# Second-type MLPs: up projections as seven products of quarter matrices, with weight sums made by accumulating DMAs

## Chip, cores and metric

The kernel runs on one core of a Trainium2 chip. The metric is the device time of one execution in microseconds (us). The engines are named as in the profile: PE multiplies matrices (PEld loads its weights), DVE, ACT and POOL do elementwise work, and SP and ACT issue DMAs. POOL issues some too in the changed kernel.

## What is computed

A block of the first type is followed by two layers of the second type, on 512 tokens with 1024 features, in float32. The change lies in the MLP of the second type:

```python
for l in range(DEPTH_2):                      # 2 layers
    ...                                       # attention, convolution, w_o
    h2 = _rmsnorm(x, g_ffn[l])
    z = _dwconv(h2 @ w_up[l], w_dw_ffn[l], b_dw_ffn[l])   # w_up: 1024 x 5632, conv of 3 taps over tokens
    zg, zv = jnp.split(z, 2, axis=-1)         # 2816 gate and 2816 value columns
    x = x + (jax.nn.silu(zg) * zv) @ w_down[l]            # w_down: 2816 x 1024
```

## The kernel before

Features lie on the 128 partitions and the 512 tokens along the free dimension: `x` is eight tiles of 128x512. A product with a weight block of 128x128 is three matmuls (`mm3`), since weights and inputs are each split into a high and a low part of the type that PE multiplies in one pass: `whi` with `xh`, `whi` with `xl`, `wlo` with `xh`.

**The weight stream.** The host packs all weights in the order of use into units of eight 128x128 blocks (`weight_plan`, `pack_weights`), 512 KB each. `take` hands out block after block. It prepares units (`prep`) up to three ahead of the one in use: SP loads `raw` (L356, three buffers), ACT casts it to `whi` (L357), POOL subtracts to get `wlo` (L358). `whi` and `wlo` have four buffers each. There are 301 units.

**The MLP.** The 22 columns of 128 gate features each pair with 128 value features. For each pair PE runs 2 projections of 8 blocks (`proj`), 48 matmuls of 512 columns. `conv3` multiplies the result by the norm's factor `r`, which is a row over tokens and so may come after the product (L1279). It then does the 3 taps (L1282 to L1284). Silu and the product of gate and value follow (L1298), then the split into `ah` and `al`. After 11 pairs (`CHUNK2`) come the 8 down projections of that chunk, each added to `x` (L1303). The first two pairs run as `proj_outer`, with four banks of PSUM open and the input tiles in the outer loop, because the inputs come one by one from the step before. The sum for the norm (`total`, L478) stands behind it, and `rsqrt` makes `r` from it (L342, L487 to L489). Layer 2's last chunk ends in `final`, which does the last two down projections in halves of 256 columns, with the last norm and the stores.

Tile pools give PSUM its eight banks in turn (`b`). A scheduler orders each engine's instructions ahead of time, and every engine runs its own in that order.

Of the kernel before, what the change touches and what calls it, by code (L numbers as in the profile page):

```python
# [39 lines left out]
NL = 2  # L40
# [6 lines left out]
CHUNK2 = 11  # L47
# [27 lines left out]
def _span(c0, n=P):  # L75
    return np.arange(c0, c0 + n)


def weight_plan():
# [47 lines left out]
    for l in range(NL):  # L127
# [31 lines left out]
        for c in range(NF2 // CHUNK2):  # L159
            fs = list(range(c * CHUNK2, (c + 1) * CHUNK2))  # L160
            if c == 0:
                add(outer("w_up_2", l, KT, [_span(P * f + o) for f in fs[:2] for o in (0, FF2)]))
                fs = fs[2:]
            for f in fs:
                add(tiles("w_up_2", l, k8, _span(P * f)))
                add(tiles("w_up_2", l, k8, _span(FF2 + P * f)))
            add([("w_down_2", l, P * k, _span(P * m)) for m in range(KT) for k in range(c * CHUNK2, (c + 1) * CHUNK2)])
# [3 lines left out]
def pack_weights(inputs, plan):  # L171
    out = np.zeros((len(plan), P, UNIT * P), np.float32)
    for u, blocks in enumerate(plan):
        for b, (name, l, r0, cols) in enumerate(blocks):
            w = inputs[name] if l is None else inputs[name][l]
# [4 lines left out]
    return out  # L180

# [70 lines left out]
class Kern:  # L252
    def __init__(self, tc, xT, w, vec, cst, pos, outT):
        self.tc, self.nc = tc, tc.nc
        self.xT, self.w, self.vec_d, self.cst_d, self.pos_d, self.outT = xT, w, vec, cst, pos, outT
        self.plan = weight_plan()
        self.units = {}
        self.prepped = 0
        self.cur, self.blk = 0, 0
        self.table, self.table_users = None, []  # L260


    def setup(self, ctx):
# [23 lines left out]
        nc.gpsimd.memset(self.epst, EPS)  # L287
        self.lna = {}
# [59 lines left out]
    def prep(self, u, eng=None):  # L348
        nc = self.nc
        n = len(self.plan[u]) * P  # L350
        raw = self.wp.tile([P, UNIT * P], F32, name="raw", bufs=3)
        hi = self.wp.tile([P, UNIT * P], FR, name="whi")
        lo = self.wp.tile([P, UNIT * P], FR, name="wlo")
        cuts = (0, n) if eng is None else (0, n // 2, n)
        for cs in map(slice, cuts, cuts[1:]):
            nc.sync.dma_start(out=raw[:, cs], in_=self.w[u, :, cs])  # L356
            nc.scalar.copy(out=hi[:, cs], in_=raw[:, cs])  # L357
            (eng or nc.gpsimd).tensor_tensor(out=lo[:, cs], in0=raw[:, cs], in1=hi[:, cs].bitcast(F32), op=ALU.subtract)  # L358
        self.units[u] = (hi, lo)

# [39 lines left out]
    def proj_outer(self, pool, tag, acts, n, parts=WHOLE, between=None):  # L400
# [3 lines left out]
        if len(parts) == 1:  # L404
            for k, a in enumerate(acts):
                for ps in pss:
                    self.mm3(ps, self.take(), a, k == 0, k == len(acts) - 1)
            return pss
# [82 lines left out]
    def norm_in(self, pool, gname, l, on_pool=KT - 2):  # L491
# [14 lines left out]
        def finish(pp, tag):  # L506
            r = self.rp.tile([P, S], F32, name="r", bufs=1)
            self.rsqrt(r, self.total(pp, tag, acc)[0], D)
            return r
# [470 lines left out]
    def layer2(self, l, carry=None):  # L980
# [294 lines left out]
        ffc = tc.tile_pool(name="ffc", bufs=CHUNK2, reuse_waits="tile")  # L1275
        fp = ffc.__enter__()

        def conv3(ps, f, tag):
            V.tensor_tensor(out=ps, in0=ps, in1=r, op=ALU.mult)  # L1279
            w3 = self.v("w_dw_ffn_2", l, 3 * f, 3)  # L1280
# [6 lines left out]
        for c in range(NF2 // CHUNK2):  # L1287
            a = []
            pss = []
            if c == 0:  # L1290
                pss = self.proj_outer(pp, "b", acts, 4)
                r = fin(pp, "b")
            for f in range(c * CHUNK2, (c + 1) * CHUNK2):
                pg, pv = pss[2 * f : 2 * f + 2] if 2 * f < len(pss) else (self.proj(pp, "b", acts), self.proj(pp, "b", acts))
                cg = conv3(pg, f, "cg")
                cv = conv3(pv, NF2 + f, "cv")
                self.act(AF.Silu, out=cg, in_=cg)
                V.tensor_tensor(out=cg, in0=cg, in1=cv, op=ALU.mult)  # L1298
                a.append(self.split(fp, cg, ("ah", "al")))
            tail = 2 if l == NL - 1 and c == NF2 // CHUNK2 - 1 else 0  # L1300
            for m in range(KT - tail):
                ps = self.proj(pp, "b", a)
                V.tensor_tensor(out=self.x[m], in0=self.x[m], in1=ps, op=ALU.add)  # L1303
            if tail:
                self.final(pp, a)
        self._close(ffc)
        self._close(xg)
        self._close(pp_)

# [39 lines left out]
def program(tc, xT, w, vec, cst, pos, outT):  # L1349
    from contextlib import ExitStack  # L1350

    with ExitStack() as ctx:
        k = Kern(tc, xT, w, vec, cst, pos, outT)
        k.setup(ctx)
        carry = k.block1()
# [5 lines left out]
def arrays(inputs):  # L1361
# [3 lines left out]
        "w": pack_weights(inputs, weight_plan()),  # L1365
        "vec": pack_vectors(inputs),
# [14 lines left out]
```

## Time and profile before

| | |
|---|---|
| median of 3 runs (range) | 1893.43 us (1893.03 to 1894.1) |
| the profiled execution | 1894.09 us, of which its span is 1892.4 us |
| PE busy | 1844.0 us, 97% of the span |
| DVE, ACT, POOL busy | 959.7, 948.1, 937.1 us, 51%, 50%, 50% |
| mean DMA rate | 87 GB/s |

Busy times of PE are those of overlapping matmuls: each is recorded with 0.39 us at 512 columns, while the next one starts earlier. So the distance of starts tells what PE needs, and the count of matmuls in a window tells how full it is. The second-type MLPs lie at 931 to 1291 us and at 1519 to 1876 us of the span.

### The profile page before, as it was taken

The numbers are of one execution on the slowest core, as the hardware profiler recorded it, in microseconds if no ns is written. First come the engines' busy times: TensorE is split into PE (matmuls) and PEld (weight loads), VectorE is DVE, ScalarE is ACT, GpSimd is POOL, SyncE is SP. The second block draws the span as 40 slices with busy tenths as digits, with TensorE's granted clock in tenths as the row PEclk, the third lists the DMA queues.
The fourth block names the chain that finished last, engine by engine and source line by source line (L and its number), as shares of the span: only waits on it lengthen the run. The fifth ranks groups of instructions, "written<-read, shape, count | busy, mean of one in ns | idle before, by whom it ended". The sixth has DMA issues, their size and how long they took to land. (4 is left out here: it accounts for less than half of the span.)

```text
span 1892.4 us, 22115 instructions
## 1 busy us (share of the span) xinstructions
PE 1844.0 (97%) x8448; PEld 1500.1 (79%) x8448; DVE 959.7 (51%) x1420; ACT 948.1 (50%) x1442; POOL 937.1 (50%) x510
## 2 busy tenths in 40 slices
PE   8999999999999999899999999999999999999997
PEld 6877888888888888666788888888866788888886
DVE  4666552724032038996565225522998365405543
ACT  6766633633233347597554224434778554324442
POOL 5233444644444558665544444455866464444442
PEclk9999999999999999999999999999999999999999
DMA  5111224222222222200232222222210122222221
GB/s 186 68 56 61 79 101 140 89 101 91 99 100 90 100 79 90 78 27 23 87 110 93 97 101 97 92 100 93 97 39 23 61 101 100 92 98 100 95 96 56
DMA packets 48649, 164.89 MB, mean 87 GB/s; under 512 B 5536, under 2 KB 7584, under 8 KB 48544
## 3 DMA queue, kind: packets, MB, share of 16 engines
q1 hardware_dynamic: 46304, 160.34, 24.5%
q10 hardware_dynamic: 2240, 3.15, 0.5%
q8 instruction: 66, 1.08, 0.2%
q14 instruction: 39, 0.32, 0.1%
HBM read 161.37 MB, written 2.10 MB: 86 GB/s over the span
## 5 line engine op out<-in xcount | busy, mean ns | idle before, releaser
L358 POOL TENSOR_TENSOR wlo<-raw,whi 128x1024 fp32r<-128x1024 f32 x300 | 720.7, 2404 | 817.5 <-ACT whi L357 813.6
L357 ACT CAST whi<-raw 128x1024 fp32r<-128x1024 f32 (+1 forms) x302 | 313.7, 1040 | 507.5 <-PE b L379 412.7
L378 PE MATMUL b<-xh,whi 128*128 128x512 f32 (+1 forms) x1296 | 495.3, 382 | 2.7 <-ACT xh L449 2.7
L379 PE MATMUL b<-xl,whi 128*128 128x512 f32 (+1 forms) x1296 | 491.7, 379 | 3.4 <-DVE xl L450 3.3
L380 PE MATMUL b<-xh,wlo 128*128 128x512 f32 (+1 forms) x1296 | 491.3, 379 | 0.0
L379 PEld LDWEIGHTS b<-xl,whi 128*128 128x128 f32 x1296 | 244.3, 189 | 51.6 <-DVE xl L450 4.4
L378 PEld LDWEIGHTS b<-xh,whi 128*128 128x128 f32 x1296 | 244.2, 188 | 50.4 <-ACT xh L449 3.1
L380 PEld LDWEIGHTS b<-xh,wlo 128*128 128x128 f32 x1296 | 244.3, 189 | 45.9
L378 PE MATMUL b<-ah,whi 128*128 128x512 f32 (+1 forms) x646 | 243.6, 377 | 0.0
L379 PE MATMUL b<-al,whi 128*128 128x512 f32 (+1 forms) x646 | 243.2, 377 | 0.0
L380 PE MATMUL b<-ah,wlo 128*128 128x512 f32 (+1 forms) x646 | 243.2, 376 | 0.0
L380 PEld LDWEIGHTS b<-ah,wlo 128*128 128x128 f32 x646 | 121.6, 188 | 22.4
L378 PEld LDWEIGHTS b<-ah,whi 128*128 128x128 f32 x646 | 121.6, 188 | 22.3
L379 PEld LDWEIGHTS b<-al,whi 128*128 128x128 f32 x646 | 121.6, 188 | 22.2
L1218 POOL TENSOR_TENSOR cacc<-cacc,pd 128x510 f32<-128x510 f32 (+14 forms) x94 | 120.4, 1281 | 32.0 <-ACT pd L1216 28.3
L1206 DVE SCALAR_TENSOR_TENSOR cv<-u,vec,cv 128x497 f32<-128x497 f32 (+13 forms) x146 | 108.3, 742 | 7.7 <-ACT cv L1196 5.5
L1279 DVE TENSOR_TENSOR b<-b,r 128x512 f32<-128x512 f32 x88 | 61.0, 697 | 97.1 <-PE b L380 96.9
L1303 DVE TENSOR_TENSOR x<-x,b 128x512 f32<-128x512 f32 x30 | 20.6, 687 | 161.3 <-PE b L380 161.3
L446 ACT CAST ah<-cg 128x512 fp32r<-128x512 f32 x44 | 27.3, 621 | 98.7 <-DVE cg L1298 98.7
L378 PE MATMUL mm<-xh,whi 128*128 128x512 f32 x176 | 69.4, 394 | 0.0
L869 DVE TENSOR_TENSOR b<-rl,b 128x512 f32<-128x512 f32 x32 | 22.1, 695 | 92.6 <-ACT rl L868 92.6
L379 PE MATMUL mm<-xl,whi 128*128 128x512 f32 x176 | 68.8, 391 | 0.0
(430 smaller groups left out, 2851.1 us busy)
## 6 DMA issues: line engine op xcount, KB each, us to landing
raw<-w SPq DMA_DIRECT2D x295, 512.0 KB, 3.2
x<-xT SPq DMA_DIRECT2D x8, 256.0 KB, 6.6
x<-xT ACTq DMA_DIRECT2D x8, 256.0 KB, 4.8
raw<-w SPq DMA_DIRECT2D x7, 256.0 KB, 2.6
outT<-o ACTq DMA_DIRECT2D x4, 256.0 KB, 2.4
outT<-o SPq DMA_DIRECT2D x4, 256.0 KB, 2.5
vec<-vec SPq DMA_DIRECT2D x1, 363.0 KB, 6.9
f<-pos SPq DMA_DIRECT2D x1, 256.0 KB, 3.3
```

What stands on the lines that cost most here:

```text
L357: nc.scalar.copy(out=hi[:, cs], in_=raw[:, cs])
L358: (eng or nc.gpsimd).tensor_tensor(out=lo[:, cs], in0=raw[:, cs], in1=hi[:, cs].bitcast(F32), op=ALU.subtract)
L378: mm(ps, lhsT=wb[0], rhs=xb[0], start=start, stop=False, **kw)
L379: mm(ps, lhsT=wb[0], rhs=xb[1], start=False, stop=False, **kw)
L380: mm(ps, lhsT=wb[1], rhs=xb[0], start=False, stop=stop, **kw)
L446: nc.scalar.copy(out=hi, in_=src)
L869: V.tensor_tensor(out=ps, in0=rl, in1=ps, op=ALU.mult)
L1206: V.scalar_tensor_tensor(out=acc[:, o], in0=us[i][:, u], scalar=self.v("w_dw_conv_2", l, i * CONV_K + k), in1=acc[:, o], op0=ALU.mult, op1 ...
L1218: G.tensor_tensor(out=acc[:, o], in0=acc[:, o], in1=pd, op=ALU.add)
L1279: V.tensor_tensor(out=ps, in0=ps, in1=r, op=ALU.mult)
L1303: V.tensor_tensor(out=self.x[m], in0=self.x[m], in1=ps, op=ALU.add)
```

## The change

For all but the first three pairs of a layer, gate and value are computed together. The weight of a pair is cut into four quarters (a11, a12, a21, a22: two halves of the 1024 inputs, gate and value), the normed input into B11 to B22 (two halves of the features, tokens 0 to 255 and 256 to 511). Seven products of 4 blocks by 256 columns and sums of them give the same four results as eight such products. Four weight sums are needed (S1 = a21 + a22, S2 = S1 + a11, S3 = a11 + a21, S4 = S2 + a12 in the signs of the packed quarters) and four input combinations (T1 to T4). The results come out with the value's sign turned, which the taps undo (`wneg`).

- **Weight sums.** They are made in DRAM, each in five regions of four pairs (the last of three): ACT issues a copy of one quarter or sum into the region, and POOL an accumulating DMA that adds another quarter. That is 80 DMAs of up to 1 MB: 40 per layer. One is issued behind the `whi` cast (copies) or the `wlo` subtraction (adds) of every second unit from unit 24 on for layer 0, then of every third unit from unit 105 on for layer 1, up to unit 222. Layer 0's quarter products begin with unit 147.
- **Weight stream.** A pair takes 28 blocks (3.5 units) where it took 16 (2 units); there are 359 units. Units that hold quarters or sums are loaded by two or more DMAs of 256 KB.
- **Inputs.** `norms` runs inside `proj_outer` before its fourth input tile; `r` is multiplied into the inputs, and `quarter_inputs` makes and splits the seven operands (14 casts on ACT, 6 subtractions on POOL, 24 instructions on DVE per layer). The first three pairs still use the plain inputs and multiply by `r` afterwards.
- **Products.** PE's order is written by hand. Between products three partial sums per pair are copied out by ACT (`snap`, 128x256) and added by DVE (`plus`, 128x256). `unit` writes into PSUM where `conv3`'s user wrote to SBUF.
- **Chunks.** Three of 8, 7 and 7 pairs instead of two of 11; the last pair's two late products stand between the first down products.

```diff
-CHUNK2 = 11
+CHUNKS2 = (0, 8, 15, 22)
+PLAIN2 = 3
+NDOWN = 3
+SUM_PAIRS = 4
+SIDE_FROM, SIDE_STEPS = 24, (2, 3)
...
+        if u >= SIDE_FROM and self.side and u % SIDE_STEPS[self.side[0][0]] == 0:
+            _, begin, on_pool = self.side.popleft()
+            self.issue_behind(begin(), rest if on_pool else cast)
...
+            def copy(dst, src):
+                return lambda: nc.scalar.dma_start(out=dst, in_=src)
+            def add(dst, src):
+                return lambda: nc.gpsimd.dma_start(out=dst, in_=src, accum_op=ALU.add, max_dma_last_dim=row)
...
+        pss = self.proj_outer(pp, "b", acts, 2 * OUTER2, between=norms)
+        pss += [self.proj(pp, "b", acts) for _ in range(2 * (PLAIN2 - OUTER2))]
...
-            V.tensor_tensor(out=ps, in0=ps, in1=r, op=ALU.mult)
...
+                def times(ps, name, start, stop):
+                    hi, lo = ops[name]
+                    for kk in range(KT // 2):
+                        self.mm3(ps, self.take(), (hi[:, kk], lo[:, kk]), ...)
+                def p4(g):
+                    times(g["v"][:, L], "T4", False, True)
+                    plus(g["v"][:, R], g["g"][:, R], g["u3"])
+                def p3(g):
+                    times(g["g"][:, R], "B22", False, True)
+                    plus(g["g"][:, R], g["g"][:, R], g["u2"])
+                    a.append(unit(g["f"], g["g"], g["v"], self.wneg[l][:, 3 * g["f"] : 3 * g["f"] + 3]))
...
+                    times(g["v"][:, L], "B11", True, False)
+                    u1 = snap(g["v"][:, L])
+                    times(g["g"][:, L], "B21", True, True)
+                    plus(g["g"][:, L], g["g"][:, L], u1)
+                    if old is not None:
+                        p4(old)
+                    times(g["v"][:, L], "T2", False, False)
+                    g["u2"] = snap(g["v"][:, L])
+                    times(g["g"][:, R], "T1", False, False)
+                    if old is not None:
+                        p3(old)
+                    times(g["v"][:, L], "T3", False, False)
+                    g["u3"] = snap(g["v"][:, L])
...
+                down(0, 4)
+                p4(old)
+                down(4, 8)
+                p3(old)
+                down(8, NDOWN * len(ks))
```

**PE, start of layer 0's MLP.** `acc_...,ones` is the norm's sum; the `b_...` are banks. Before, with the last of the outer projections ahead of it and the third pair behind:

```order
L380 MATMUL b_7870<-xh_7825,wlo_7874 128x512
L378 MATMUL b_7871<-xh_7825,whi_7873 128x512
L379 MATMUL b_7871<-xl_7826,whi_7873 128x512
L380 MATMUL b_7871<-xh_7825,wlo_7874 128x512
L478 MATMUL b_7993<-acc_7810,ones_115 128x512
L378 MATMUL b_8034<-xh_7811,whi_7903 128x512
```

Now:

```order
L478 MATMUL b_7987<-xh_7914,whi_7838 128x512
L479 MATMUL b_7987<-xl_7915,whi_7838 128x512
L480 MATMUL b_7987<-xh_7914,wlo_7839 128x512
L580 MATMUL b_8038<-acc_7909,ones_115 128x512
L478 MATMUL b_7984<-xh_7916,whi_7838 128x512
L479 MATMUL b_7984<-xl_7917,whi_7838 128x512
```

The sum moved from behind all 96 matmuls of the outer projections to behind the first 36 of them.

**DVE, the same place,** from the last step of `rsqrt` on. Before (layer 1's, which has the same shape) it goes over to the first pair at once:

```order
L489 SCALAR_TENSOR_TENSOR r_12561<-b_12562,r_12561 128x512
L1279 TENSOR_TENSOR b_12437<-b_12437,r_12561 128x512
L1279 TENSOR_TENSOR b_12438<-b_12438,r_12561 128x512
L1279 TENSOR_TENSOR b_12439<-b_12439,r_12561 128x512
L1283 SCALAR_TENSOR_TENSOR cg_12571<-b_12437,vec_67,cg_12571 128x511
```

Now (layer 0), the second half of `quarter_inputs` and what follows it, where `t`, `h0`, `h1` are the inputs' tiles and L1437 is the first `plus`:

```order
L1534 SCALAR_TENSOR_TENSOR t_8086<-t_8086,h1_8077 128x512
L1426 TENSOR_TENSOR b_7984<-b_7984,r_8037 128x512
L1426 TENSOR_TENSOR b_7985<-b_7985,r_8037 128x512
L1518 TENSOR_TENSOR T4l_7978<-t_8086,T4h_7977 128x512
L1426 TENSOR_TENSOR b_7986<-b_7986,r_8037 128x512
L1426 TENSOR_TENSOR b_7987<-b_7987,r_8037 128x512
L1426 TENSOR_TENSOR b_8175<-b_8175,r_8037 128x512
L1426 TENSOR_TENSOR b_8207<-b_8207,r_8037 128x512
L1404 SCALAR_TENSOR_TENSOR cg_8248<-b_7984,vec_67,cg_8248 128x511
L1404 SCALAR_TENSOR_TENSOR cv_8252<-b_7985,vec_67,cv_8252 128x511
L1437 TENSOR_TENSOR b_8296<-b_8296,snap_8317 128x256
```

Between `rsqrt` and the first `plus` of the first quarter pair DVE now has the 24 instructions of `quarter_inputs`, the six multiplications by `r` of the plain pairs and two taps.

**POOL, layer 0's last chunk.** Before there are only subtractions:

```order
L358 TENSOR_TENSOR wlo_8193<-raw_8191,whi_8192 128x1024
L358 TENSOR_TENSOR wlo_8224<-raw_8222,whi_8223 128x1024
L358 TENSOR_TENSOR wlo_8271<-raw_8269,whi_8270 128x1024
L358 TENSOR_TENSOR wlo_8302<-raw_8300,whi_8301 128x1024
L358 TENSOR_TENSOR wlo_8349<-raw_8347,whi_8348 128x1024
```

Now, with the adds for layer 1's sum S4:

```order
L404 TENSOR_TENSOR wlo_10742<-raw_10740,whi_10741 128x1024
L449 DMA S4_1_2_169<-wq 512x512
L404 TENSOR_TENSOR wlo_10780<-raw_10778,whi_10779 128x1024
L404 TENSOR_TENSOR wlo_10813<-raw_10811,whi_10812 128x1024
L404 TENSOR_TENSOR wlo_10846<-raw_10844,whi_10845 128x1024
L449 DMA S4_1_3_173<-wq 512x512
```

Every third subtraction is followed by an accumulating DMA of 512 rows of 512 numbers, which POOL issues before the next subtraction.

## Rows read from the trace of the kernel before

**Rows 1.** The page: busy time of each engine, its share, instructions.

```profile
PE 1844.0 (97%) x8448; PEld 1500.1 (79%) x8448; DVE 959.7 (51%) x1420; ACT 948.1 (50%) x1442; POOL 937.1 (50%) x510
```

**Rows 2.** Windows: layer 0's MLP, its up phase, layer 1's MLP; length, busy (count), clock, DMA.

```profile
core 0: us, PE busy (x) PEld busy (x) DVE busy (x) ACT busy (x) POOL busy (x), PEclk, DMA share, GB/s
931.30:1291.00 359.70, 359.70 (x1586) 297.57 (x1585) 157.77 (x211) 143.06 (x179) 172.99 (x76) 1.00 0.28 97
969.00:1051.00 82.00, 82.00 (x363) 67.92 (x362) 48.63 (x68) 37.36 (x49) 36.09 (x15) 1.00 0.28 97
...
1502.00:1862.00 360.00, 360.00 (x1588) 297.71 (x1587) 162.71 (x214) 146.17 (x184) 169.14 (x72) 1.00 0.27 94
```

**Rows 3.** Timeline of PE, first block: matmuls of 256 columns (start, length, what).

```profile
328.75 0.28 PE L378 MATMUL b<-mh,whi 128*128 128x256 f32 x1
...
330.79 0.28 PE L380 MATMUL b<-mh,wlo 128*128 128x256 f32 x1
330.91 0.28 PE L378 MATMUL b<-mh,whi 128*128 128x256 f32 x1
```

**Rows 4.** Groups by line with shapes apart: count, busy us, mean ns, idle before.

```profile
L357 ACT CAST whi<-raw 128x1024 fp32r<-128x1024 f32 x295 | 309.4, 1051 | 506.0 <-PE b L379 412.7 <-issue 44.7 <-PE mm L379 20.6
L358 POOL TENSOR_TENSOR wlo<-raw,whi 128x1024 fp32r<-128x1024 f32 x295 | 714.1, 2423 | 802.1 <-ACT whi L357 802.0
L358 POOL TENSOR_TENSOR wlo<-raw,whi 128x512 fp32r<-128x512 f32 x5 | 6.6, 1316 | 15.4 <-ACT whi L357 11.6 <-ACT ph L1156 3.8
L460 ACT ACTIVATE sq<-x 128x256 f32<-128x256 f32 x31 | 12.6, 407 | 8.9 <-DVE x L1329 6.6 <-POOL acc L461 2.0
L532 DVE TENSOR_TENSOR x<-x,b 128x256 f32<-128x256 f32 x32 | 13.3, 416 | 0.7
L447 DVE TENSOR_TENSOR al<-cg,ah 128x512 fp32r<-128x512 f32 x44 | 30.4, 691 | 26.2 <-ACT ah L446 26.1
```

**Rows 5.** DMA issues: count, size, median us to landing.

```profile
raw<-w SPq DMA_DIRECT2D x295, 512.0 KB, 3.2
raw<-w SPq DMA_DIRECT2D x7, 256.0 KB, 2.6
```

**Rows 6.** Windows: the first loads, when DMA engines are full; block 1 and attention.

```profile
60.00:620.00 560.00, 549.86 (x2640) 460.87 (x2639) 245.86 (x335) 273.23 (x427) 240.31 (x116) 1.00 0.26 90
...
4.00:16.00 12.00, 10.12 (x33) 7.89 (x34) 7.27 (x9) 9.21 (x16) 2.41 (x1) 1.00 0.99 360
```

**Rows 7.** Timeline at the start of layer 0's MLP: the sum's inputs, the sum, `rsqrt`.

```profile
939.62 0.68 DVE L461 TENSOR_TENSOR acc<-acc,sq 128x512 f32<-128x512 f32 x1
...
953.09 1.02 PE L478 MATMUL b<-acc,ones 128*128 128x512 f32 x2
953.55 0.79 PE L378 MATMUL b<-xh,whi 128*128 128x512 f32 x1
...
957.10 0.69 DVE L489 SCALAR_TENSOR_TENSOR r<-b,r 128x512 f32<-128x512 f32 x1
957.89 1.90 DVE L1279 TENSOR_TENSOR b<-b,r 128x512 f32<-128x512 f32 x3
959.70 0.74 DVE L1283 SCALAR_TENSOR_TENSOR cg<-b,vec,cg 128x511 f32<-128x511 f32 x1
960.35 0.74 DVE L1283 SCALAR_TENSOR_TENSOR cv<-b,vec,cv 128x511 f32<-128x511 f32 x1
```

**Rows 8.** Timeline of DVE and POOL side by side there: both read SBUF.

```profile
931.55 5.17 DVE L450 SCALAR_TENSOR_TENSOR xl<-x,vec,xh 128x512 fp32r<-128x512 f32 x3
...
932.86 3.32 POOL L461 TENSOR_TENSOR acc<-acc,sq 128x512 f32<-128x512 f32 x2
```

**Rows 9.** Timeline of SP: one DMA issue.

```profile
956.66 0.33 SPq L356 DMA_DIRECT2D raw<-w  x1
```

**Rows 10.** Timeline at the end: last matmul; DVE's stores of the first half, then the rest.

```profile
1880.62 0.28 PE L380 MATMUL b<-ah,wlo 128*128 128x256 f32 x1
...
1877.83 3.19 DVE L1338 TENSOR_TENSOR o<-x,f 128x256 f32<-128x256 f32 x6
...
1881.28 0.41 DVE L1329 TENSOR_TENSOR x<-x,b 128x256 f32<-128x256 f32 x1
```

More of the change, by code (lines that the diff above doesn't have):

```diff
@@ L76, in _span, with chunks2 @@
     return np.arange(c0, c0 + n)
+def chunks2():
+    return [range(a, b) for a, b in zip(CHUNKS2, CHUNKS2[1:])]
 def weight_plan():
@@ L180, in pack_weights, with pack_quarters @@
     return out
+def pack_quarters(inputs):
+    w = inputs["w_up_2"].reshape(NL, 2, KT // 2, P, 2, NF2, P)[:, :, :, :, :, PLAIN2:]
+    w = w.transpose(0, 4, 1, 5, 3, 2, 6)
+    return np.ascontiguousarray(w).reshape(NL, 4, NF2 - PLAIN2, P, KT // 2 * P)
 def vector_plan():
@@ L287, in setup @@
         nc.gpsimd.memset(self.epst, EPS)
+        self.wneg = {}
+        for l in range(NL):
+            t = c.tile([P, 3 * NF2], F32, name=f"wneg{l}")
+            nc.gpsimd.tensor_scalar(out=t, in0=self.v("w_dw_ffn_2", l, 3 * NF2, 3 * NF2), scalar1=-1.0, scalar2=None, op0=ALU.mult)
+            self.wneg[l] = t
         self.lna = {}
@@ L353, in prep @@
         lo = self.wp.tile([P, UNIT * P], FR, name="wlo")
[L354 to L358, printed above, removed]
-        self.units[u] = (hi, lo)
+        if eng is None and any(b[0] in QUARTERS + SUMS for b in self.plan[u]):
+            for c0, c1, src in self.sources(u):
+                nc.sync.dma_start(out=raw[:, c0:c1], in_=src)
+            cuts = ((0, n),)
+        else:
+            cuts = ((0, n),) if eng is None else ((0, n // 2), (n // 2, n))
+            for c0, c1 in cuts:
+                nc.sync.dma_start(out=raw[:, c0:c1], in_=self.w[u, :, c0:c1])
@@ L405, in proj_outer @@
             for k, a in enumerate(acts):
+                if k == OUTER_LAG + 2 and between is not None:
+                    between()
                 for ps in pss:
@@ L504, in split, with finish @@
                 self.sq_add(acc[:, cs], x, i == 0, nc.gpsimd if i < on_pool else nc.vector)
-        def finish(pp, tag):
+        def finish(pp, tag, both=False):
             r = self.rp.tile([P, S], F32, name="r", bufs=1)
-            self.rsqrt(r, self.total(pp, tag, acc)[0], D)
-            return r
+            tot = self.total(pp, tag, acc)[0]
+            if not both:
+                self.rsqrt(r, tot, D)
+                return r
+            self.rsqrt(r, tot, D, tot)
+            nc.scalar.copy(out=r, in_=tot)
+            return r, tot
         return acts, split, finish
@@ L1285, in conv3, with unit @@
             return c
[L1287 to L1305, printed above, removed]
+        def unit(f, pg, pv, wv):
+            cg = conv3(pg, self.v("w_dw_ffn_2", l, 3 * f, 3), f, "cg")
+            cv = conv3(pv, wv, NF2 + f, "cv")
+            self.act(AF.Silu, out=pg, in_=cg)
+            V.tensor_tensor(out=pg, in0=pg, in1=cv, op=ALU.mult)
+            return self.split(fp, pg, ("ah", "al"))
@@ L1346, in final, with program @@
             norm(HALVES[1])
-def program(tc, xT, w, vec, cst, pos, outT):
+def program(tc, xT, w, wq, vec, cst, pos, outT):
     from contextlib import ExitStack
     with ExitStack() as ctx:
-        k = Kern(tc, xT, w, vec, cst, pos, outT)
+        k = Kern(tc, xT, w, wq, vec, cst, pos, outT)
         k.setup(ctx)
+        k.sums(ctx)
         carry = k.block1()
@@ L1365, in arrays @@
         "w": pack_weights(inputs, weight_plan()),
+        "wq": pack_quarters(inputs),
         "vec": pack_vectors(inputs),
```

171 lines of the change are left out of this document (157 added, 14 removed).

## Prediction

> **What bounds the kernel now.** I read the page's busy line first [rows 1]: PE is busy 97% of the span, the other three engines half of it. So a step counts only where it gives PE fewer columns to multiply or makes PE wait. Next the windows of the two MLPs [rows 2]. Layer 0's holds 1586 matmuls in 359.70 us, which is 0.2268 us for each 512 columns, at a granted clock of 1.00, and layer 1's the same (1588 in 360.0). That is PE without a gap, so nothing in these MLPs waits for weights or for DVE, and fewer columns would be time saved one to one, as long as everything else keeps up. Third, what 256 columns cost: the timeline of PE in block 1 has 18 steps from 328.75 to 330.91, 0.120 us each [rows 3]. Two of them are 0.240, so halving a matmul costs 6%.
>
> The profiled execution took 1894.09 us; the median is 0.7 us less. The sum below is made against the profiled time; the difference is smaller than its rounding, and the forecast is given against the median.
>
> **What PE saves.** A pair had 48 matmuls of 512 columns, 48 x 0.2268 = 10.89 us. It gets 7 x 4 x 3 = 84 of 256, 84 x 0.120 = 10.08 us. The saving is 0.81 us for each of 19 pairs in 2 layers: 38 x 0.81 = **-30.6 us**. So seven products instead of eight give 7.4% of a pair, not 12.5%. The rest goes to the smaller matmuls, and 31 us is all that the other parts may eat.
>
> A rule bears on this term. The Trainium skill, page "TensorE: Matmul & The Clock Gate", section "Back-to-back issue gap", gives the isolated gap at the full clock as N/2.4 + 2.5 ns: 109 ns for 256 columns and 216 for 512, and it holds longer matmuls to be faster still in a stream. By its formula a pair would go from 10.36 to 9.17 us, an estimate of -45 us in place of -30.6. The rows have 0.227 and 0.120 us, above it in both shapes, so the rows decide.
>
> **The start of each MLP.** Now `total` stands behind 36 matmuls. PE is there at 931.3 + 36 x 0.227 = 939.5, but `acc` has its last addend at 939.62 + 0.68 = 940.3 [rows 7]. PE stands for 0.8 us. From `total` to the end of `rsqrt` it was 953.09 to 957.79, so `r` comes at about 945.0. From there DVE has the 24 instructions of `quarter_inputs`, then six multiplications by `r`, two taps and the first `plus`. PE's product with T1 goes into the bank that this `plus` works on, so it waits for it.
>
> - Eight products with `r` in PSUM at 0.65 (the spacing at 959.70 and 960.35 [rows 7]) = 5.2 us; sixteen instructions with two SBUF inputs at 0.69 [rows 4] = 11.0.
> - POOL's six subtractions of 512 columns at 1.316 [rows 4] = 7.9, and a `wlo` of 2.42 among them. The rows show that DVE and POOL don't run freely side by side here: three DVE instructions that each take 0.74 alone took 5.17 while POOL did two in 3.32 [rows 8]; 3 x 0.74 + 3.32 = 5.5, nearly one after the other. So I add them: 5.2 + 11.0 + 7.9 + 2.4 = 26.5, less some 3 us in which DVE reads PSUM: 23.5. That ends at about 969 to 971.
> - Six multiplications at 1.90/3 [rows 7] = 3.8, two taps 1.3, `plus` 0.42 (the 256-column add [rows 4]): 5.5. T1 may start at 974 to 977.
>
> PE gets there at 931.3 + 96 x 0.227 + 0.46 for `total` + 0.8 + 10.9 for the third pair + 3 x 1.44 = 969.6. It waits 4.4 to 7.4, say 6; with the 0.8, 6.8 a layer: **+13.6 us**. The ends: with no contention DVE is through at 966.7 and only the 0.8 is left (1.6 in all); with no overlap at all, and the second pair waiting for banks as well, 12 a layer (24).
>
> **Between the products.** A partial sum that ACT copies out or DVE adds is needed two products later, 2.88 us. The answer is a copy or add of 0.41 [rows 4], at worst behind one cast of 1.05, and the hops between engines: 1.8 us, inside 2.88. In a pair's 10.08 us ACT has about 7.7 us of work, DVE 5.6, POOL 3.5 x 2.42 = 8.5. I take **+1**; if a snap is sometimes behind two casts, 0.3 a pair, 11.
>
> **The stream of weights** goes faster: a unit of 24 matmuls lasted 5.44 us (15 `wlo` in the 82 us window [rows 2]) and lasts 2.88 now. A `raw` buffer goes round in 3.2 us to land [rows 5] (2.6 where it is 256 KB), plus a second issue of 0.33 [rows 9], a cast of 1.05, a subtraction of 2.42 and hops: 7.0 for three units' 8.64. It holds, with 1.6 us to spare, and POOL has 8.64 - 3 x 2.42 = 1.38 to spare. Nothing.
>
> **Chunk ends and the tail.** One more chunk end a layer, where the last pair's conversion, some 7 us, has 7 to 9 us of down products for cover: **+2** (0 to 6). In layer 1's last chunk a down projection has 7 inputs instead of 11, so the last two have 2 x 4 x 3 x 0.12 = 2.9 us less of PE work. DVE's stores of the first half start at 1877.83 and end at 1881.02 [rows 10], 0.4 us after the last matmul at 1880.62, so this chain comes to the front: **+2.5** (0 to 3).
>
> **The sums.** Layer 0's forty DMAs are issued in units of 5.4 us, where POOL is busy 240 of 560 us [rows 6]: hidden. Layer 1's S1 falls mostly into attention, likewise hidden. But layer 1's other adds, units 150 to 162, 180 to 192 and 210 to 222, all lie in quarter products of layer 0, one in three units, with 11 copies between. The kernel before has no DMA issued by POOL. Its hold on POOL is 0.33 by the row of an SP issue [rows 9], which would be free beside the 1.38 to spare. If POOL is held as long as 1 MB read twice takes at the rate of full DMA engines, 360 GB/s [rows 6], it is 5.8, and then (5.8 - 1.38) x 15 = 66, less some 5 us of lead in each of three runs: 51. I take 1.5, nearer to the issue row, because an issue is what a queue does. On the DMA engines, three units' loads and a copy are 2.6 MB, 7.3 us at that rate; with an add that reads twice, 10.2, over 8.64 by 1.5; 15 x 1.5 = 23, again less the lead. They also make `raw` land later, against its 1.6 to spare. I take **+4** in all (0 to 51).
>
> **Sum:** -30.6 + 13.6 + 1 + 2 + 2.5 + 4 = -7.5. **1886 us.**
>
> **Rivals.**
>
> *A, the starts are covered.* If DVE's and POOL's work overlaps better than in [rows 8], T1 is ready before PE, 12 us come back, and the time is about 1874. For it: DVE's products read `r` from PSUM, and POOL's subtractions wait for ACT's casts, so they needn't meet. Against it: sixteen of 24 instructions read two SBUF tensors.
>
> *B, the adds hold the stream (slower).* Place: layer 0's quarter products, units 150 to 222. POOL waits while it issues an add, or the add takes so much of the DMA engines that `raw` lands late; either way `wlo` comes late and PE stops. Each add above POOL's 1.38 us costs PE the rest, less the lead. The point is worked out without the +4: the other terms leave -11.5, so 26.5 us in 15 adds turn the sign, which is a hold of 1.38 + 1.77 = 3.1 us. At 5.2 us, most of the way to the full transfer, it is (5.2 - 1.38) x 15 - 15 = 42, 1893.4 - 11.5 + 42 = 1924; midway between 3.1 and that, 1908. For it: DMA share is 0.28 at 97 GB/s before [rows 2], and would nearly double with the faster stream before any sum. Against it: no row shows POOL held by an issue.
>
> The Trainium skill, page "DMA: Bandwidth & Descriptors", section "Anatomy of one DMA — SWDGE (gpsimd) path", puts a GpSimd-issued DMA at 2.0 us plus bytes/436e3, with most of the 2 us spent waiting for the write's receipt and generation of descriptors called small. Worked out, 1 MB would take an estimated 4.4 us, mostly not on POOL, which speaks against a long hold. No run here shows it yet.
>
> *C, the handshakes cost too.* The starts cost their upper end (24) or the copies between products 0.3 a pair; the saving is gone: 1896. For it: ACT has 7.7 of 10.08 us, in whatever order the scheduler put it. It lies between A's and B's sides, within the noise or a little above.
>
> **How the numbers follow.** Forecast (sum about right, 1880 to 1893): 0.40; A: 0.20; C: 0.14; B: 0.26. A measurement of this kernel can tell about 0.2%, 3.8 us, from no change. Of the forecast's 0.40, 0.30 is faster than 1889.6 and 0.10 within; A's 0.20 is faster; C gives 0.10 within and 0.04 slower; B is slower. Faster 0.50, same 0.20, slower 0.30. The range takes A's value and a little below, and B's middle and a little above: 1870 to 1915, with about 0.07 left below and 0.12 above. The likeliest case's own range is 1880 to 1893.
>
> **What would show it.** Matmuls of 256 columns 0.120 us apart in layer 0's and layer 1's quarter products; if 0.113 or less, the saving was undersized, if 0.125, over half of it is gone (84 x 0.005 x 38 = 16). One idle stretch of PE of some 6 us before the first T1 of each layer that ends on DVE's `plus`: if absent, A. POOL's idle time and the distance of `wlo` around its DMAs in layer 0's chunks, beside the same in layer 1's, which has no sums: equal times say B is wrong; a longer layer 0 gives its size. Snaps and adds as releasers of PE within pairs: C. At the end, the stores' chain after the last matmul: about 2.5 us longer. Most likely to break the forecast is the price of the adds, the one operation of which the trace has no row.

## Result: slower, 1917.5 us

| | before | changed |
|---|---|---|
| median (runs) | 1893.76 us (4) | 1917.51 us (4) |
| profiled execution, span | 1894.09, 1892.4 us | 1919.48, 1917.8 us |
| ratio of times, 95% interval | | 1.0127 [1.0108, 1.0147] |

The forecast was 1886 us, in a range of 1870 to 1915. The kernel became 23.8 us slower instead of 7.5 faster. It went the way of rival B, a little beyond the range.

### The profile page after: what moved, and what is told of

It is laid out like the page before. It is cut to its first block, busy times and chain, and to the rows that moved or that the text cites. A ratio compares the mean times of both kernels' runs of the same rounds, so it can differ in the third digit from the quotient of the medians.

```text
span 1917.8 us, 25905 instructions
## 1 busy us (share of the span) xinstructions
PE 1829.8 (95%) x9792; PEld 1538.0 (80%) x9792; DVE 1013.4 (53%) x1522; ACT 1050.1 (55%) x1644; POOL 1134.3 (59%) x622
## 3 DMA queue, kind: packets, MB, share of 16 engines
q0 software_dynamic: 20096, 39.85, 11.7%
## 5 line engine op out<-in xcount | busy, mean ns | idle before, releaser
L404 POOL TENSOR_TENSOR wlo<-raw,whi 128x1024 fp32r<-128x1024 f32 (+1 forms) x358 | 862.5, 2419 | 638.6 <-ACT whi L403 630.3
L403 ACT CAST whi<-raw 128x1024 fp32r<-128x1024 f32 (+1 forms) x360 | 373.6, 1040 | 504.0 <-PE b L479 340.0
L479 PE MATMUL b<-xl,whi 128*128 128x512 f32 (+1 forms) x688 | 257.7, 375 | 7.1 <-DVE xl L552 7.0
L478 PE MATMUL b<-xh,whi 128*128 128x512 f32 (+1 forms) x688 | 261.0, 379 | 2.7 <-ACT xh L551 2.7
L480 PE MATMUL b<-xh,wlo 128*128 128x512 f32 (+1 forms) x688 | 256.9, 373 | 0.0
L479 PEld LDWEIGHTS b<-xl,whi 128*128 128x128 f32 x688 | 129.9, 189 | 34.9 <-DVE xl L552 8.5
L478 PEld LDWEIGHTS b<-xh,whi 128*128 128x128 f32 x688 | 129.7, 189 | 29.7 <-ACT xh L551 3.1
L480 PEld LDWEIGHTS b<-xh,wlo 128*128 128x128 f32 x688 | 129.8, 189 | 25.0
L1437 DVE TENSOR_TENSOR b<-b,snap 128x256 f32<-128x256 f32 x114 | 48.8, 428 | 79.7 <-PE b L480 69.2
L549 DVE TENSOR_TENSOR al<-b,ah 128x512 fp32r<-128x512 f32 x76 | 52.3, 690 | 56.4 <-ACT ah L548 56.3
L480 PE MATMUL mm<-xh,wlo 128*128 128x512 f32 x176 | 69.5, 395 | 0.0
## 6 DMA issues: line engine op xcount, KB each, us to landing
S<-wq POOLq DMA_DIRECT2D x32, 1024.0 KB, 10.9
```

The lines of the kernel that those rows point to most:

```text
L403: cast = nc.scalar.copy(out=hi[:, cs], in_=raw[:, cs])
L404: rest = (eng or nc.gpsimd).tensor_tensor(out=lo[:, cs], in0=raw[:, cs], in1=hi[:, cs].bitcast(F32), op=ALU.subtract)
L478: mm(ps, lhsT=wb[0], rhs=xb[0], start=start, stop=False, **kw)
L479: mm(ps, lhsT=wb[0], rhs=xb[1], start=False, stop=False, **kw)
L480: mm(ps, lhsT=wb[1], rhs=xb[0], start=False, stop=stop, **kw)
L549: self.last_lo = (lo_eng or nc.vector).tensor_tensor(out=lo, in0=src, in1=hi.bitcast(F32), op=ALU.subtract)
```

## The profile after

First the lines of the page that answer to [rows 1] and [rows 5]: busy times, then what the DMA queues took (packets, MB, share of 16 engines' span; q0 is POOL's, q10 ACT's), and the sums' DMAs (count, size, us to landing).

```profile
PE 1829.8 (95%) x9792; PEld 1538.0 (80%) x9792; DVE 1013.4 (53%) x1522; ACT 1050.1 (55%) x1644; POOL 1134.3 (59%) x622
...
q0 software_dynamic: 20096, 39.85, 11.7%
q10 hardware_dynamic: 3520, 42.99, 6.3%
...
S<-wq POOLq DMA_DIRECT2D x32, 1024.0 KB, 10.9
```

An add takes 11.7% of 1917.8 us / 40 = 5.6 us of all DMA engines on average (32 of the 40 move 1 MB, 8 move 768 KB). A copy takes about 2.8: the 6.3% less the 0.5% that q10 takes in e1, where it has no copies, again over 40.

Next a table by stage. The windows run from the start to the first MLP of the second type, over that MLP, to the next, over that, and to the end. Columns are the window, its length, PE busy (matmuls), granted clock, DMA share, GB/s. Before:

```profile
0.00:931.30 931.30, 901.59 (x4270) 0.99 0.25 87
931.30:1291.00 359.70, 359.70 (x1586) 1.00 0.28 97
1291.00:1519.50 228.50, 219.88 (x936) 0.99 0.18 62
1519.50:1880.60 361.10, 361.10 (x1654) 1.00 0.26 90
1880.60:1892.40 11.80, 1.70 (x7) 0.68 0.50 164
```

The changed kernel:

```profile
0.00:941.10 941.10, 909.36 (x4271) 0.99 0.48 143
941.10:1323.00 381.90, 353.24 (x2270) 0.96 0.69 201
1323.00:1555.20 232.20, 223.71 (x936) 0.99 0.18 62
1555.20:1902.80 347.60, 341.50 (x2314) 0.99 0.41 136
1902.80:1917.80 15.00, 1.94 (x7) 0.64 0.41 140
```

Stage by stage that is +9.8, +22.2, +3.7, -13.5 and +3.2 us. The two MLPs run the same products, and only layer 0's has sums beside it: it takes 34 us longer than layer 1's. Layer 1's alone became 13.5 faster. And two stretches whose PE work the change doesn't touch became 13.5 slower together.

**Layer 0's MLP.** Here is what PE waited for between 990 and 1290 us, and below it what ACT waited for (us in total, times, longest):

```profile
PE b L478 <- ACT snap L1432: 13.3, 6, 3.6
PE b L478 <- DVE b L1437: 8.9, 3, 3.7
```

```profile
ACT whi L403 <- DMA raw<-wq: 27.1, 10, 5.3
ACT whi L403 <- DMA raw<-S: 19.7, 9, 4.0
...
ACT whi L403 <- DMA raw<-w: 9.3, 4, 4.0
```

None of PE's waits in this stretch is for a weight. It waited for a copy between products (`snap`), or for DVE's addition of one. In the same stretch ACT stood 56 us for loads. One such wait, in the timeline of the engines around 1113 us (start, length, engine, operation, then in brackets the idle time and what ended it):

```profile
1112.48 1.04 ACT L403 CAST whi<-raw 128x1024 fp32r<-128x1024 f32 x1 [3.99 <-DMA raw<-S]
...
1114.11 0.36 ACT L1432 COPY snap<-b 128x256 f32<-128x256 f32 x1
...
1114.52 0.19 PEld L478 LDWEIGHTS b<-T3h,whi 128*128 128x128 f32 x1 [2.76 <-ACT snap L1432]
```

ACT has the cast of a unit that PE needs only later, and stands 3.99 us for its load. The `snap` that PE needs at once stands behind it in ACT's queue, with one of ACT's taps (L1403) between them. So the lead of the weight stream doesn't protect PE. In DMA issues from 1104 to 1140 us the loads are late (size, median us to landing):

```profile
S<-wq POOLq DMA_DIRECT2D x4, 1024.0 KB, 11.2
raw<-S SPq DMA_DIRECT2D x12, 256.0 KB, 5.7
raw<-wq SPq DMA_DIRECT2D x8, 256.0 KB, 4.1
```

In layer 1's last chunk, 1790 to 1860 us, without sums, they aren't:

```profile
raw<-S SPq DMA_DIRECT2D x23, 256.0 KB, 2.9
raw<-wq SPq DMA_DIRECT2D x16, 256.0 KB, 2.8
```

**PE's step.** The second surprise is in the distance of matmul starts. In the timeline of PE at 540 us, in a product of block 1 that both kernels have, before:

```profile
539.91 0.39 PE L378 MATMUL b<-xh,whi 128*128 128x512 f32 x1
...
545.13 0.39 PE L380 MATMUL b<-xh,wlo 128*128 128x512 f32 x1
```

After:

```profile
539.63 0.39 PE L478 MATMUL b<-xh,whi 128*128 128x512 f32 x1
...
544.76 0.39 PE L479 MATMUL b<-xl,whi 128*128 128x512 f32 x1
```

Before it is 23 steps in 5.22 us, 0.227 each, after 22 in 5.13, 0.233, with PE busy throughout. In the quarter products the step differs from what [rows 3] showed as well. These are layer 1's second and third chunk (windows as above):

```profile
1689.00:1753.00 64.00, 64.00 (x561) 1.00 0.57 182
...
1794.00:1861.00 67.00, 67.00 (x569) 1.00 0.54 180
```

That is 0.1141 and 0.1178 us a matmul instead of 0.120. From start to start the steps are 0.1134 in the one and 0.1177 in the other; the first chunk has two gaps of about 0.1 us at its beginning.

## Experiments

The first four ask what the sums cost and by what. **e1** leaves out all of their DMAs:

```diff
-                src = self.sum_of[l, name, reg]...[i * P : (i + 1) * P]
+                src = self.wq[l, SUMS.index(name), f - PLAIN2]
```

> Leaves out all 80 sum DMAs (copies and adds); where a product would load a sum it loads one of the plain quarters, the same bytes. So the products with sums are computed with other weights. Layer 0's MLP (first matmul with xh to last with ah) takes 382.2 us in the changed kernel and 347.7 in layer 1, which has no sum DMAs beside it. Theory D (the sums' DMAs cost it): layer 0 falls to about 348, the whole to about 1917.5 - 35 = 1882, give or take 6 for the steps of PE outside the MLPs. Rival Q (the quarter products of layer 0 are slow for another reason, such as their loads in halves): layer 0 stays near 380, the whole within 5 us of 1917.

Measured: 1884.35 us, 0.995 [0.9934, 0.9967] of before; layer 0's MLP 350.7 us instead of 381.9. Theory D holds: the sums cost 33 us. But the stretch ahead of the MLPs took 938.3 us: 7.0 of its 9.8 us stayed, without any sum.

**e2** leaves out the adds alone:

```diff
-                    self.side.append((l, add(self.sum_of[l, name, g], quarter(more, r)), True))
+                    self.side.append((l, None, True))
```

> The 40 adds are left out, so the sums are only copies of one term; the 40 copies by ACT stay at their places. By the page the adds take 11.7% of 16 engines' span (224 us, 5.6 each), the copies 6.3% (3.0 each). Theory D (the DMA engines are full): three units' loads and a copy are 4.4 + 3.0 = 7.4 us of the 8.64 that three units have, so layer 0's MLP takes 348 to 352 us, the whole 1883 to 1889. Rival: the copies' 64 KB pieces hold up the loads behind them: layer 0 stays above 362.

Measured: 1885.2 us, layer 0's MLP 345.7. That is one run, within a microsecond of e1. The copies cost nothing that can be told from noise; it is the adds.

**e3** keeps POOL's DMAs, but lets them write:

```diff
-                return lambda: nc.gpsimd.dma_start(out=dst, in_=src, accum_op=ALU.add, max_dma_last_dim=row)
+                return lambda: nc.gpsimd.dma_start(out=dst, in_=src, max_dma_last_dim=row)
```

> The 40 DMAs by POOL stay, with the same source, size, 2 KB rows and issue, but write instead of adding (so the sums hold one term only). Theory D: without the second read an add costs what a copy costs, about 3 us of full engines in place of 5.6, and three units fit their 8.64 us: layer 0's MLP 348 to 358 us, the whole 1883 to 1895. Rival P (POOL's issue, 1.0 us at each, or the making of 512 rows' descriptors, holds the stream): POOL is held as before, layer 0 stays at 375 or more, the whole above 1910.

Measured: 1903.5 us, layer 0's MLP 367.0. Both lie between the two expectations. POOL's queue took 5.2% of 16 engines instead of 11.7%, so less than half of the DMA time removes 14 of the 33 us. POOL's hold isn't what was left: its issue took 0.6 us here (1.0 with the add) and the next `wlo` followed as soon as its cast was there. A load issued right behind such a DMA (at 1116.85 us, behind the one of 1116.38) landed 5.8 us after its issue instead of 2.9. The mean share of the DMA engines around it was 0.75, but they were full just then (windows, with PE's matmuls):

```profile
1118.00:1122.00 4.00, 4.00 (x38) 1.00 1.02 384
1112.00:1140.00 28.00, 23.16 (x199) 1.00 0.75 259
```

So a plain write of 1 MB still fills the engines for some 5 us and makes the load behind it late, though there is time enough between two of them. That fits what was left of the cost.

**e4** moves layer 1's sums out of layer 0's MLP:

```diff
-SIDE_FROM, SIDE_STEPS = 24, (2, 3)
+SIDE_AT = [*range(24, 104, 2), *range(104, 144, 2), *range(237, 257)]
...
-        if u >= SIDE_FROM and self.side and u % SIDE_STEPS[self.side[0][0]] == 0:
+        if u in SIDE_AT:
```

> All 80 DMAs stay, and the result is the same; layer 1's are issued at every second unit from 104 to 142 (S1, S3) and at every unit from 237 to 256 (S2, S4, in layer 1's attention), so none stands in layer 0's MLP. Theory D: layer 0's MLP takes about 348 us; in attention the DMA engines were 17% busy, and PE asks for few weights there, so at most some 5 us come back: the whole 1882 to 1890, faster than the kernel before. Rival: the cost of a sum goes with it wherever it stands (POOL is busy with the convolution there): the stretch between the MLPs grows by 20 or more and the whole stays above 1902.

Measured: 1890.33 us, 0.9984 [0.9974, 0.9993]; layer 0's MLP 348.0, as layer 1's, and the stretch between the MLPs 236.3 instead of 232.2. As theory D has it: beside attention the sums cost 4 us, beside the quarter products 34.

Then PE's step. I matched each matmul with the addresses that the built program gives its tiles. Before, inputs and weights agree modulo 512 bytes in 6448 steps of 512 columns, nearly all, mean 0.2270 us. The change adds two constant tiles of 264 bytes (`wneg`), which move the weights and most tiles by 576 bytes, while pools at the top of SBUF stay. In the changed kernel 2426 steps agree, mean 0.2270, and in 2189 the input lies 64 bytes below the weight modulo 512, mean 0.2333. Three runs test this.

**e6** makes the constant tiles 512 bytes wide, on top of e4:

```diff
-            t = c.tile([P, 3 * NF2], F32, name=f"wneg{l}")
+            t = c.tile([P, 128], F32, name=f"wneg{l}")[:, : 3 * NF2]
```

> e4_moved_sums with the two constant tiles wneg made 512 bytes wide (they are 264), so that the weight tiles, which lie behind them, agree with the inputs at the top of SBUF modulo 512 again, as in the kernel before. Theory A: all steps are 0.2267 and 0.120; up to the first second-type MLP 9 us less than e4 (942 to 933), between the MLPs 3 less, each MLP 7 us more (348 to 355): the whole about 2 more than e4, 1888 to 1896. Rival S: nothing changes, each stretch within 1.5 us of e4.

Measured: 1894.4 us, 1.0004 [0.9994, 1.0013] of before. Its windows are

```profile
0.00:931.50 931.50, 900.09 (x4271) 1.00 0.53 151
931.50:1287.10 355.60, 347.45 (x2271) 0.99 0.47 148
1287.10:1521.60 234.50, 222.41 (x937) 0.98 0.51 137
1521.60:1878.20 356.60, 348.92 (x2316) 0.99 0.43 133
```

and the timeline of PE in a quarter product of layer 1 shows the step of [rows 3]:

```profile
1700.03 0.28 PE L478 MATMUL b<-T4h,whi 128*128 128x256 f32 x1
...
1700.87 0.28 PE L479 MATMUL b<-T4l,whi 128*128 128x256 f32 x1
```

Theory A, in each stretch: 942.4 to 931.5, 348.0 to 355.6, 236.3 to 234.5, 348.5 to 356.6. The shift cost the 512-column matmuls and helped the 256-column ones.

**e12** gives the kernel before nothing but the two tiles:

```diff
+        for l in range(NL):
+            t = c.tile([P, 3 * NF2], F32, name=f"wneg{l}")
+            nc.gpsimd.tensor_scalar(out=t, in0=..., scalar1=-1.0, scalar2=None, op0=ALU.mult)
```

> The kernel before, with nothing of the change but the two constant tiles of 264 bytes that it adds ahead of the weight tiles in SBUF (filled, and not used). Theory A: the matmuls whose inputs lie at the top of SBUF go from 0.2267 to 0.2333; up to the first second-type MLP 9 us more, between the MLPs 3 more, the MLPs unchanged: 1903 to 1907, slower than the kernel before. Rival (that slowdown of the changed kernel came from its DMAs or its code): within 1.5 us of the kernel before.

Measured: 1905.26 us, 1.0061 [1.0044, 1.0078]. Its windows:

```profile
0.00:940.00 940.00, 910.72 (x4270) 0.99 0.26 87
940.00:1299.70 359.70, 359.70 (x1586) 1.00 0.29 97
1299.70:1531.10 231.40, 222.90 (x937) 0.99 0.18 61
1531.10:1892.30 361.20, 361.20 (x1655) 1.00 0.27 90
```

Two unused tiles cost 11.7 us: 8.7 ahead of the MLPs, 2.9 between them, nothing in them, where inputs and weights moved together.

**e5** spreads the addresses, on top of e4 (`xh` and `xl` likewise):

```diff
-tuple(pool.tile([P, KT // 2, S // 2], FR, name=n + part) for part in "hl")
+tuple(pool.tile([P, n4 + 16], FR, name=n + part)[:, :n4].rearrange("p (k c) -> p k c", k=KT // 2) for part in "hl")
```

> The kernel with moved sums (e4_moved_sums), whose second-type MLP inputs (the eight pairs xh, xl and the fourteen quarter operands) each lie 64 bytes further on in SBUF than the one before allows, so that their distances from the weights run through all steps of 64 bytes within 512. In the changed kernel each matmul of 512 columns starts 0.2267 us after the one before where input and weight addresses agree modulo 512, and 0.2333 where they differ by 64; of 256 columns 0.120 and 0.1134 to 0.1175. Theory A (the distance of the two addresses sets the step): in this run the step differs from operand to operand, with the operands that agree modulo 512 at 0.2267 and 0.120. Rival S (the step is left behind by the last wait of PE, as 0.1134 after a wait and 0.1175 without one): no order by operand, all of one chunk alike.

Measured: 1898.8 us. The step differs by operand. Of 512 columns: 0.2271 where two successive matmuls both agree, 0.229 to 0.234 at all other distances. Of 256: 0.1197 where both agree, 0.1153 from distance 128 to 64, 0.1198 from 64 to 64, nearly all others between. A distance is the input's address less the weight's, modulo 512; that of the changed kernel is 448, and from 448 to 448 it was 0.1175 here. So agreeing is best for 512 columns. For 256 columns I found no rule.

**e11** tries why one chunk ran at 0.1141 and the next at 0.1178, at the same addresses:

```diff
+                    if (l, f) == (1, 15):
+                        times(g["g"][:, L], "B21", True, True)
                     times(g["v"][:, L], "B11", True, False)
                     u1 = snap(g["v"][:, L])
-                    times(g["g"][:, L], "B21", True, True)
+                    if (l, f) != (1, 15):
+                        times(g["g"][:, L], "B21", True, True)
```

> e9_combined with the first two products of one pair exchanged (layer 1, pair 15, the first of its last chunk): B21 first, then B11, whose copy by ACT the next product needs at once, so PE waits some 0.7 us there. Before, that chunk ran without a wait at 0.1175 a matmul, the chunk ahead of it, which began with two waits of about 0.1 us, at 0.1134, with the same operands and addresses. Theory S (within one placement the step is left behind by the last wait): the last chunk's 564 products fall to 0.1134, 2.3 us less for 0.7 us of wait. Rival: they stay at 0.1175, and the chunk is 0.7 us longer.

Measured: 1873.7 us. PE waited 1.5 us there, and the chunk's step stayed at 0.1178. In the changed kernel's layer 0, though, the last chunk ran at 0.1177 up to PE's first wait in it (2.2 us, at 1234 us) and at 0.1134 behind it. So a wait may change the step and need not. In e9 the chunk ahead of it ran at 0.1178 too, with the same short waits as in this run, where it ran at 0.114. My theory that the last wait sets the step is wrong; what chooses between the two is open.

Then the ways from a late load to PE. **e7** gives `raw` a fourth buffer, in the changed kernel:

```diff
-        raw = self.wp.tile([P, UNIT * P], F32, name="raw", bufs=3)
+        raw = self.wp.tile([P, UNIT * P], F32, name="raw", bufs=4)
```

> The changed kernel with four buffers for the loaded weights instead of three, sums where they were. In the changed kernel a load behind an add lands after 6 to 8 us instead of 3, and the DMA engines are 91 to 100% busy in those stretches. Theory L (lateness: the ring of three can't cover a late load, while there would be time enough on average): layer 0's MLP falls from 382 to 360 or less, the whole below 1896. Theory D (the engines are full, so no buffer helps for long): layer 0's MLP stays above 372, the whole above 1907.

Measured: 1897.5 us, layer 0's MLP 357.1. The MLP is inside theory L's bound of 360 and 15 us below D's; the whole is 1.5 us above L's bound of 1896 and 9.5 below D's. PE's waits from 990 to 1290 us:

```profile
PE b L478 <- ACT snap L1432: 4.9, 5, 1.9
PE b L478 <- DVE b L1437: 1.7, 3, 0.7
```

In the stretch where the changed kernel's share of the DMA engines was 0.92, they were now full:

```profile
1104.00:1140.00 36.00, 34.42 (x296) 1.00 1.09 289
```

Over the whole MLP the share was 0.74, so the engines had time enough on average. A load that is issued one buffer earlier may be late without stopping ACT, and 25 of the 34 us went with that. The other 9 stayed.

**e13** lets DVE make the copies between products:

```diff
-                        A.copy(out=t, in_=ps)
+                        V.tensor_copy(out=t, in_=ps)
```

> The changed kernel, sums where they were, with the copies between the products (snap) made by DVE instead of ACT. In the changed kernel every wait of PE in layer 0's quarter products ended on a snap (13.3 us) or on DVE's add of one (8.9), none on a weight; at the waits ACT stood at the cast of a late load with the snap queued behind it. Theory Q (the late load reaches PE through ACT's queue): the 13.3 us on ACT's snap go; those through DVE, which waits for ACT's taps, may stay or grow somewhat: layer 0's MLP falls from 382 to 360 to 372. Theory L2 (the late load is missed as a weight soon after anyway): the waits move to whi and wlo, layer 0's MLP stays at 378 or more.

Measured: 1913.5 us, layer 0's MLP 373.5, between the two. PE's waits there:

```profile
PE b L478 <- DVE b L1437: 11.3, 6, 3.5
PE b L478 <- DVE snap L1432: 6.7, 4, 2.9
```

No wait is for a weight in this run either, so L2 falls. But DVE itself waits for ACT's taps, which stand behind the same casts (38.5 us in this stretch), so the copies are still late: the queue theory is right on the way, and 8 us is all that moving one of its links brings.

Last, the start and the sum of it all. **e8**, on top of e4:

```diff
-            put("B11", b11, G)
-            put("B21", b21, G)
+            put("B11", b11, V)
+            put("B21", b21, V)
...
-            put("B22", b22, G)
+            put("B22", b22, V)
```

> e4_moved_sums with the six subtractions of the quarter inputs that POOL did (B11, B21, B22) done by DVE. Theory K (DVE and POOL take turns, as in rows 8: in layer 1's start some 10 us of DVE's time went beyond its alone-durations): DVE gets 6 x 0.69 = 4.1 us more work but loses up to 7.9 us of turns: PE's wait before the first T2 falls from 5 or 6 us to 1 to 4, the whole 4 to 8 us below e4. Rival W (DVE simply has too much to do): the wait grows by 3 to 4 us a layer, the whole 6 to 9 above e4.

Measured: 1881.9 us; the MLPs took 343.4 and 343.0 instead of 348.0 and 348.5. The whole is 8.4 us below e4, a little more than theory K's 4 to 8; W falls. In the changed kernel's layer 1 the start looks so, first PE, then DVE with POOL beside it, then ACT:

```profile
1592.18 0.28 PE L480 MATMUL b<-B21h,wlo 128*128 128x256 f32 x1
1598.13 0.58 PE L478 MATMUL b<-T2h,whi 128*128 128x256 f32 x1 [5.67 <-ACT snap L1432]
...
1598.73 0.41 PE L480 MATMUL b<-T2h,wlo 128*128 128x256 f32 x1
1598.94 0.41 PE L478 MATMUL b<-T2h,whi 128*128 128x256 f32 x1
```

```profile
1591.98 2.35 POOL L404 TENSOR_TENSOR wlo<-raw,whi 128x1024 fp32r<-128x1024 f32 x1 [2.83 <-ACT whi L403]
...
1592.02 2.85 DVE L1534 SCALAR_TENSOR_TENSOR t<-t,h 128x512 f32<-128x512 f32 x1
1594.80 1.28 DVE L1426 TENSOR_TENSOR b<-b,r 128x512 f32<-128x512 f32 x2
```

```profile
1596.38 0.77 ACT L1403 ACTIVATE cg<-b,vec 128x512 f32<-128x512 f32 x1
...
1597.71 0.37 ACT L1432 COPY snap<-b 128x256 f32<-128x256 f32 x1
```

The instruction of DVE at 1592.02 takes 2.85 us, ending just behind a `wlo` of POOL that began ahead of it; the same instruction takes 0.68 where POOL is idle (e8, at 1558.37 us). The last of the six multiplications by `r` follow late, ACT's taps wait for them, and `snap` stands behind the taps. After its 5.67 us without work PE goes on at 0.21 us a matmul (1598.73 to 1598.94), nearly twice the step, which is the lower of the two clock levels (1.2 instead of 2.4 GHz), up to 1603 us; the granted clock from 1590 to 1605 us is 0.77. In e4 this wait is 7.1 us in each layer; in e8 it is

```profile
PE b L478 <- ACT snap L1432: 2.3, 1, 2.3
```

**e9** puts e4, e6 and e8 together, and moves the quarter operands by 64 bytes so that they alone differ from the weights:

```diff
+        pool.tile([P, 16], F32, name="pad")
```

> All that the runs so far point to, in one kernel with the same result: sums moved out of layer 0's MLP (e4), start on DVE (e8), constants of 512 bytes (e6), and the quarter operands moved down by 64 bytes, so that only they differ from the weights by 64 modulo 512. If the parts add: the stretch up to the first second-type MLP about 931, each MLP about 343, between them 234, the whole 1866 to 1873, over 1% faster than the kernel before. Rival: the parts don't add (a wait that one took away comes back in another place): 1876 or more.

Measured: 1871.47 us, 0.9889 [0.9874, 0.9904] of the kernel before. The time lies in the range for parts that add. In the profiled execution, the slowest of the four (1875.88 us), the MLPs took 346.9 and 345.4 us instead of 343, with more chunks at 0.1178 than in e8. No other version was faster.

**e10** adds the fourth buffer:

> e9_combined with four buffers for the loaded weights. If late loads still cost something (in e4 the stretch between the MLPs, where the moved sums now stand, was 4 us longer than in the changed kernel): 2 to 5 us less than e9, 1862 to 1870. Rival (three buffers are enough once the sums are out of the MLP, and the 4 us came from POOL or ACT): within 1 us of e9.

Measured: 1871.97 us, 0.9888 [0.9873, 0.9903], no more than e9. Once the sums are out of the MLP three buffers are enough.

**e14** adds DVE's snaps to e9:

> e9_combined with the snaps made by DVE. There the sums are away, loads land in time and PE waits only at the MLPs' starts, 2.3 us on a snap in each. Theory: snaps on DVE stand behind the same six multiplications, so the start gains at most 1 us each; elsewhere nothing: within 3 us of e9 (1869 to 1874). Rival (ACT's queue is still the limit in the whole MLP): 4 us or more faster. Other rival (DVE, now with 7 of 10 us busy per pair, is late with its adds): slower than 1875.

Measured: 1878.96 us, 0.9931 [0.9915, 0.9948], slower than e9 and in the range of the second rival. That DVE's adds come late isn't shown, though. In the profiled execution each MLP's waits are about 1.5 us longer. But that execution took as long as e9's (1875.95 and 1875.88 us), so the two traces can't show where the difference of the medians lies.

## Why the prediction was wrong

| term | predicted | measured |
|---|---|---|
| PE, 38 pairs | -30.6 | about -46 |
| starts | +13.6 | +18 |
| between products | +1 | 0 without sums |
| chunk ends | +2 | 0 |
| tail | +2.5 | +3.2 |
| sums | +4 (0 to 51) | +33 to +38 |
| placement in SBUF | not seen | +11.7 |

The measured column adds to about +20 to +25; the kernel became 23.8 slower. The misses partly cancel: PE saved 15 us more than forecast, against some 30 for the sums and 12 for the placement, so that the time lies only 2.5 us outside the range is luck.

- **The sums** are the step that failed: a term of +4 that measured 33 to 38. The working had 10.2 us of DMA time where three units have 8.64, 23 us over 15 adds, and the add's 5.6 us of engines was in it (1 MB read twice at 360 GB/s is 5.8). I then took away a lead of 5 us a group and chose +4, near the issue row. With three buffers no run shows that lead. ACT casts and copies in one queue, so a late load for a later unit holds the copy that PE needs now. I named that queue for the copies between products, and priced it with loads that come in time. That the 23 comes near the measured waits is in part chance, too: in e7 the same adds, with the engines full, cost 8 us (layer 0's MLP 357.1, layer 1's 349.3), since a fourth buffer covers most late loads. Of the 34 us between the two MLPs, waits of PE make about 25. Behind the longer waits matmuls of 256 columns start 0.21 us apart for a while, the lower clock level as shown under e8; against 0.1134 that adds 14 us in layer 0's MLP and 3 in layer 1's (granted clock 0.96 and 0.99). e1 gives 33 us; e1's own products ran 5 us slower than those of the changed kernel, so 38 is the other end.
- **POOL's hold** was the wrong half of rival B: 1.0 us an add, inside the 1.38. The other half, the load that lands late, was right: 1.6 us were to spare, and landings rose by 1.3 to 2.8 in the median, and to 9.6 at worst (990 to 1290 us). But B had the way to PE wrong: it expected PE to stop for a late `wlo`, and PE stopped for `snap` and `plus`. By the Trainium skill, page "DMA: Bandwidth & Descriptors", section "Anatomy of one DMA — SWDGE (gpsimd) path", an add was to take an estimated 4.4 us and little of POOL; the trace agrees on POOL (1.0 us) and not on the time: 10.9 us in the median beside the loads, 7.5 at the least.
- **PE's saving** was undersized by 15 us: the row of 0.120 was from a stage in which inputs and weights agree modulo 512. The quarter operands don't, by accident, and run at 0.1141 to 0.1178. e6 makes them agree, and the 0.120 is back. The rule of the Trainium skill, page "TensorE: Matmul & The Clock Gate", section "Back-to-back issue gap", gave -45, near the measured saving, though neither of its two gaps agrees with a row (0.109 and 0.216 against 0.114 to 0.118 and 0.227).
- **The placement** was outside of all cases: 11.7 us by two small constant tiles, which no reading of instructions shows.
- **The starts** went by the mechanism that I gave. The wait fell on T2 instead of T1, by way of `snap` behind ACT's taps, at 5.7 us in layer 1 where 6 was forecast; the lower clock after it added some 2 us there. e8 shows that with POOL's six subtractions on DVE the MLP is 5 us a layer shorter.
- **Between products, chunk ends, tail:** without sums, once layer 1's first T2 has begun, PE waits for nothing over 0.15 us up to its last chunk's down products. The tail is 3.2 us longer, as reasoned from [rows 10].

Rival A's time was reached only by e9 and its variants, which are different kernels. Rival C's sign did appear, snaps and adds as releasers of PE within pairs: 22.2 us of waits in layer 0's MLP. It could not tell C from B, though. Behind the first T2, the same products have no such waits in layer 1, and none in e4's layer 0, where no sums stand beside them, so they come from the adds and C's cause is out.

## To carry to other kernels

A prefetch distance protects an engine only as far as nothing else that it needs stands in a queue behind the prefetched work: look at what is queued behind each instruction that may wait for a DMA. When an estimate over capacity comes out (10.2 us in 8.64), don't subtract a cushion for which there is no row. After a change, compare PE's step in a stage that it doesn't touch: if that moved, tiles moved.

## What was new about the hardware

- The distance of matmul starts depends on where input and weights lie in SBUF; by what mechanism isn't shown. With 512 columns it is 0.227 us where both agree modulo 512 bytes and 0.233 where the input lies 64 below the weight; with 256 columns 0.120 and 0.114 to 0.118. e12 and e6 show both directions. At other distances the 256-column step was 0.115 to 0.120 (e5), and which of two steps a chunk takes at the same addresses is open.
- An accumulating DMA between places in DRAM, of 1 MB or 768 KB in rows of 2 KB, takes 5.6 us of the 16 engines on average (a copy 2.8), and holds POOL for 1.0 us (0.6 without the addition).
- A load issued right behind a POOL DMA of 1 MB can land 3 us later (5.8 instead of 2.9 us in e3). The engines were full while it was under way (1.02), though only 75% busy over the 28 us around it: a mean share hides such a burst. How the queues share the engines wasn't tried.
